# Expert numbers worked out from positions, and one-hot tiles with the row number innermost

## The chip, the cores and the metric

The kernel runs on one core of one Trainium2 chip. The metric is the time in microseconds that the device takes for one execution of the whole program; lower is better. The engines are named as the profile names them: PE is TensorE's matmuls and PEld its weight loads, DVE is VectorE, ACT is ScalarE, POOL is GpSimd (here it only issues gathers while the experts run), SP is SyncE, which issues most plain transfers.

## What is computed

The reference is a two-layer trunk over 512 tokens of width 1024. Each layer has a mixer, which the change leaves alone, and then a layer of experts ("PEER"): 8 heads, each of which picks 16 of 16384 one-neuron experts for every token.

```python
s = jnp.einsum('thpd,hpnd->thpn', q, keys32)               # 8 heads x 2 halves x 128 keys
s1_v, s1_i = lax.top_k(s[:, :, 0, :], 16)
s2_v, s2_i = lax.top_k(s[:, :, 1, :], 16)
cand_v = s1_v[..., :, None] + s2_v[..., None, :]           # 16 x 16 candidates
cand_i = s1_i[..., :, None] * 128 + s2_i[..., None, :]
top_v, top_j = lax.top_k(cand_v.reshape(..., 256), 16)
idx = jnp.take_along_axis(cand_i, top_j, axis=-1)          # 16 expert numbers per head
gate = jax.nn.softmax(top_v, axis=-1)
act = jax.nn.gelu(einsum('thkd,td->thk', u_tab[idx], hb))
out = einsum('thk,thkd->td', gate * act, v_tab[idx])
```

## The kernel before

The tokens stand in four blocks of 128. For the first three blocks (384 tokens) the experts are computed densely: every row of `u` is multiplied with every token, the result is weighted with a gate that is zero for experts not picked, and multiplied with every row of `v`. For the last block the picked rows are gathered from HBM.

**Scores.** `scores(p, ps)` finds, for each of 16 head halves and each token block, the 16 best of 128 keys (`top16`, DVE), with values in `sv` and key numbers in `sx`.

**Selection.** `select(tb)` forms, for the 8 heads of a block, the 50 candidates that can be among the best 16 (list `CAND`: 16 for the best first key, 8 for the second, and so on; `COFF` has the position at which each run begins), values in `cv` and expert numbers in `ci`. `top16` on `cv` gives values `tv` and positions `tj`. The expert number at a position is then looked up one at a time: for each of 8 heads and 16 places one DVE instruction compares a row of 50 position numbers (`iof`) with the position, multiplies with `ci` and sums (line 855, tile `jk`, 128 a block). The sum is split into first and second key number by a shift and a mask. A softmax gives the gate. For blocks 0 to 2 the three tables (first key, second key, gate) are transposed by PE (`pc`) and kept in 16 bits as `slot` and `gh` (the gate in a high and a low part).

**Build.** `build(tb, sel, g8)` makes the dense gate of four tokens. DVE writes one-hot tiles of 128 rows by 128 numbers by 4 tokens, the token innermost: `P` (first key), `Qo` (second key), and two tiles `Q`, which are `Qo` times each part of the gate. PE then multiplies, for each token, `P[:, :, t]` (as weights) with `Q[:, :, t]`, so both are read with a step of four elements: 8 matmuls a group of four tokens (lines 912 and 913), 96 groups a layer. ACT copies the result into `stg`, and every 48 tokens `stg` is written to HBM (`sW`).

**U and V.** `dense_U(i)` multiplies 128 rows of `u` with the 384 tokens: `load_split` brings 512 KB, ACT rounds it (`whi`), DVE takes the rest (`wlo`, line 116), PE makes 24 matmuls of 384 columns (lines 132 to 134), ACT applies GELU (`uo`), and 192 KB go to HBM (`sA`). 128 of these run a layer. After them the working pool `rp` is closed and pool `vp` opened in its place; then for each of 128 groups `A` and `W` are read back, multiplied (DVE), split (`gh`, `gl`), and PE makes 24 matmuls with `v` (lines 1020 to 1022).

**Gathers.** For the last block POOL issues 128 gathers of `u` rows and then 128 of `v` rows, 512 KB each, into three buffers `gr`. DVE consumes each with one instruction of 1024 columns (line 946 for `u`, line 957, tile `gacc`, for `v`). The gathers need `select(3)`, whose numbers become `idi`.

**Order.** The program is written as loops (`select(tb)`, then 32 builds, with a `dense_U` and a gather step at every second one), but a scheduler in the build sets the final order of each engine's instructions ahead of time by its own model of durations. On the chip every engine takes its instructions in that fixed order.

Of the kernel before, what the change touches and what calls it, by code (L numbers as in the profile page):

```python
# [16 lines left out]
T = 512  # L17
# [19 lines left out]
CAND = [16, 8, 5, 4, 3, 2, 2, 2] + [1] * 8  # L37
NCAND = sum(CAND)
COFF = [sum(CAND[:i]) for i in range(16)]


def trunk(tc, a, dbg=None, layers=L, n_i2=128):
    nc = tc.nc
    V, S, G, TE = nc.vector, nc.scalar, nc.gpsimd, nc.tensor
    uid = [0]

    def nm(s):
        uid[0] += 1
        return f"{s}{uid[0]}"
# [3 lines left out]
    cst = ctx.enter_context(tc.tile_pool(name="cst", bufs=1))  # L53
# [19 lines left out]
    it = ctmp.tile([128, 128], I32, name="it")  # L73
# [7 lines left out]
    V.tensor_copy(io4, it[:, :, None].to_broadcast([128, 128, 4]))  # L81
# [400 lines left out]
    def mixer(l, h):  # L482
# [4 lines left out]
        fx = hctx.enter_context(tc.tile_pool(name=f"fx{l}", bufs=1))  # L487
# [8 lines left out]
        G.memset(toe, 0.0)  # L496
        s5_maps(l, sm, fx, hp, ("w1", "w2", "w3"))
        pk0 = pack_tile(fx)
        dcol = fx.tile([128, 32], F32, name=nm("dcol"))
        for j in range(4):  # L500
            nc.sync.dma_start(dcol[32 * j:32 * j + 32, :], a["dsk"][l])
# [227 lines left out]
        fx = mctx.enter_context(tc.tile_pool(name=f"gx{l}", bufs=1))  # L729
# [13 lines left out]
        for e in range(J):  # L743
            ps = proj(40 + e)
# [15 lines left out]
        for e in range(J):  # L760
            later(3)
            ps = dense(a["glu"][l, e], ya)
# [35 lines left out]
    def peer(l, h, rows, gp):  # L798
        pctx = ExitStack()
        rp = pctx.enter_context(tc.tile_pool(name=f"rp{l}", bufs=2))  # L800
# [11 lines left out]
        def scores(p, ps):  # L812
# [9 lines left out]
            for tb in range(NB):  # L822
                wk = rp.tile([128, 128], F32, tag="wk", name=nm("wk"))
                top16(sv[:, tb, p], sx[:, tb, p], s[:, tb], wk)

        def select(tb):
            val = sv[:, tb].rearrange("p (h s) k -> p h s k", s=2)
            idf = rp.tile([128, 16, 16], F32, tag="idf", name=nm("idf"), bufs=1)
            V.tensor_copy(idf, sx[:, tb])
            idv = idf[:].rearrange("p (h s) k -> p h s k", s=2)  # L830
            V.tensor_scalar(idv[:, :, 0, :], idv[:, :, 0, :], 128.0, None, op0=OP.mult)
            cv = rp.tile([128, 8, NCAND], F32, tag="cv", name=nm("cv"), bufs=1)
            ci = rp.tile([128, 8, NCAND], F32, tag="ci", name=nm("ci"), bufs=1)
            for src, dst in ((val, cv), (idv, ci)):
                for r in range(5):
                    n = CAND[r]
                    V.tensor_tensor(dst[:, :, COFF[r]:COFF[r] + n], src[:, :, 0, r:r + 1].to_broadcast([128, 8, n]),
                                    src[:, :, 1, 0:n], op=OP.add)
                V.tensor_tensor(dst[:, :, COFF[5]:COFF[8]].rearrange("p h (r b) -> p h r b", b=2),
                                src[:, :, 0, 5:8, None].to_broadcast([128, 8, 3, 2]),  # L840
                                src[:, :, 1, None, 0:2].to_broadcast([128, 8, 3, 2]), op=OP.add)
                V.tensor_tensor(dst[:, :, COFF[8]:], src[:, :, 0, 8:16],
                                src[:, :, 1, 0:1].to_broadcast([128, 8, 8]), op=OP.add)
            tv = rp.tile([128, 8, 16], F32, tag="tv", name=nm("tv"), bufs=1)
            tj = rp.tile([128, 8, 16], U32, tag="tj", name=nm("tj"), bufs=1)
            for hh in range(8):
                wk = rp.tile([128, NCAND], F32, tag="wk2", name=nm("wk2"))
                top16(tv[:, hh], tj[:, hh], cv[:, hh], wk)
            tf = rp.tile([128, 8, 16], F32, tag="tf", name=nm("tf"), bufs=1)
            V.tensor_copy(tf, tj)  # L850
            code = rp.tile([128, 8, 16], F32, tag="code", name=nm("code"), bufs=1)
# [5 lines left out]
            cint = rp.tile([128, 128], I32, tag="cint", name=nm("cint"), bufs=1)  # L857
            V.tensor_copy(cint, code[:].rearrange("p h k -> p (h k)"))
            ii = rp.tile([128, 2, 128], I32, tag="ii", name=nm("ii"), bufs=1)
            V.tensor_scalar(ii[:, 0], cint, 7, None, op0=OP.logical_shift_right)  # L860
            V.tensor_scalar(ii[:, 1], cint, 127, None, op0=OP.bitwise_and)
            fx = rp.tile([128, 3, 128], F32, tag="fx", name=nm("fx"), bufs=1)
            V.tensor_copy(fx[:, 0:2], ii)

            gv = fx[:, 2].rearrange("p (h k) -> p h k", h=8)
            V.tensor_tensor(gv, tv, tv[:, :, 0:1].to_broadcast([128, 8, 16]), op=OP.subtract)
            S.activation(fx[:, 2], fx[:, 2], AF.Exp)
            zs = rp.tile([128, 8], F32, tag="zs", name=nm("zs"), bufs=1)
            V.tensor_reduce(zs, gv, axis=mybir.AxisListType.X, op=OP.add)
            V.reciprocal(zs, zs)  # L870
            V.scalar_tensor_tensor(gv, gv, GATE, zs[:, :, None].to_broadcast([128, 8, 16]), op0=OP.mult, op1=OP.mult)
            if tb == NB - 1:
                return fx
            pt = ptile([128, 3, 128], "pc")
            for i in range(3):
                TE.transpose(pt[:, i], fx[:, i], ident)
            st = rp.tile([128, 2, 128], F16, tag="slot", name=nm("slot"))
            S.activation(st, pt[:, 0:2], AF.Copy)
            gh = rp.tile([128, 2, 128], F16, tag="gh", name=nm("gh"))
            V.tensor_copy(gh[:, 0], pt[:, 2])  # L880
            V.tensor_tensor(gh[:, 1], pt[:, 2], gh[:, 0], op=OP.subtract)
            return st, gh

        stg = {}
# [1 line left out]
        def build(tb, sel, g8):  # L886
            st, gh = sel
            NT = 4
            c = slice(NT * g8, NT * g8 + NT)
            t0 = 128 * tb + NT * g8  # L890
            n, o = divmod(t0, SG)
            if o == 0:
                stg[0] = rp.tile([128, 128, SG], F32, tag="stg", name=nm("stg"), bufs=2)
            sh = [128, 128, NT]

            def row(t):
                return t[:, None, :].to_broadcast(sh)
# [5 lines left out]
            Qs = []  # L903
            for i in range(2):
                q = rp.tile(sh, F16, tag=f"Q{i}", name=nm("Q"))
                V.tensor_tensor(q, Q_, row(gh[:, i, c]), op=OP.mult)  # L906
                Qs.append(q)
            for b in range(NT // 4):
                ps = ptile([128, 4, 128], "pa")
                for k in range(4):  # L910
                    t = 4 * b + k
                    TE.matmul(ps[:, k], P_[:, :, t], Qs[0][:, :, t], start=True, stop=False)  # L912
                    TE.matmul(ps[:, k], P_[:, :, t], Qs[1][:, :, t], start=False, stop=True)  # L913
# [125 lines left out]
        for i in range(n_end):  # L1039
            w, g = spilled(i)  # L1040
# [31 lines left out]
    for k in ("adab", "n1g", "n2g", "glub"):  # L1072
        sh = a[k].shape
# [51 lines left out]
    for l in range(layers):  # L1125
        h = norm_mod(gain1[l], shift1[l], ssq, G if l == 0 else None)
# [72 lines left out]
```

## Time and profile before

| | us |
|---|---|
| median of 3 runs | 3928.33 (3924.42 to 3931.42) |
| the profiled execution | 3930.45 |
| its span, first to last instruction | 3928.7 |
| PE busy, by the page | 3736.3 |
| DVE busy | 3238.6 |
| ACT busy | 1574.6 |
| POOL busy | 1021.7 |
| data moved | 911.37 MB, mean 232 GB/s |

The two layers look alike: mixer until about 650 us, scores until 770, then a stretch in which U, the selections, the builds and the gathers run together until about 1365, an end of it in which only builds are left, and V from 1436 to 1985; the second layer repeats this some 1935 us later. A matmul's busy time in the profile overlaps with the next one's, so what a matmul costs PE is read from one start to the next. The same holds for DVE instructions that follow each other without a wait. The share "DMA" of a stretch is the mean busy share of the core's 16 DMA engines.

### The profile page before, as it was taken

How to read it: one execution, taken by the hardware profiler on the slowest of the kernel's cores; microseconds unless marked ns; L12 is line 12 of the kernel's file. 1: busy time of each engine (PE TensorE's matmuls, PEld its weight loads, DVE VectorE, ACT ScalarE, POOL GpSimd, SP SyncE). 2: the span in 40 equal slices, each digit the busy share in tenths (PEclk: the TensorE clock that was granted, in tenths of full speed). 3: DMA queues.
4: the chain of work that ended last, by engine and by line, in shares of the span. 5: the costliest groups of instructions: out<-in, count | busy, mean ns of one | idle time of the engine just before them, and what ended most of it. 6: DMA issues, size and time to landing. Idle time of an engine off the chain costs nothing.

```text
span 3928.7 us, 62542 instructions
## 1 busy us (share of the span) xinstructions
PE 3736.3 (95%) x21878; PEld 3502.1 (89%) x21878; DVE 3238.6 (82%) x8715; ACT 1574.6 (40%) x2507; POOL 1021.7 (26%) x1475
## 2 busy tenths in 40 slices
PE   6999999999999959999999999999999997699998
PEld 5888878999999959999988887789999997699998
DVE  6998787999898879877578886679998888787874
ACT  3554443333343323333345554344333433233332
POOL 7454100013222344221033440000232223432210
PEclk9999999999999969999999999999999998899999
DMA  5222384379998989998622225524898898999984
GB/s 197 74 64 78 102 266 143 111 249 318 326 315 304 322 300 351 348 344 315 208 85 75 71 81 168 187 84 136 303 309 315 310 325 289 333 353 344 347 294 134
DMA packets 368764, 911.37 MB, mean 232 GB/s; under 512 B 35824, under 2 KB 187440, under 8 KB 368448
## 3 DMA queue, kind: packets, MB, share of 16 engines
q1 hardware_dynamic: 247696, 536.56, 40.6%
q0 software_dynamic: 73952, 268.56, 19.7%
q10 hardware_dynamic: 46800, 102.26, 6.8%
q8 instruction: 172, 2.82, 0.3%
q14 instruction: 144, 1.18, 0.1%
HBM read 796.09 MB, written 111.15 MB: 231 GB/s over the span
## 4 chain that ended last, share of the span: by engine, by line
PE 77%; DVE 11%; DMA 7%; POOL 2%; issue 2%; ACT 1%; SPq 0%; ACTq 0%; DVEq 0%; POOLq 0%
PE mm L132 12%; PE mm L133 12%; PE mm L134 12%; PE mm L1021 3%; PE mm L1020 3%; PE mm L1022 3%; PE pb L1021 2%; PE pa L1022 2%; PE pb L1020 2%; PE pa L1021 2%; PE pa L1020 2%; PE pb L1022 2%; DMA ada<-ada 2%; DVE wlo L116 2%; PE pa L912 2%; PE pa L913 2%
## 5 line engine op out<-in xcount | busy, mean ns | idle before, releaser
L114 ACT ACTIVATE whi<-raw 128x1024 fp32r<-128x1024 f32 x688 | 728.4, 1060 | 1289.0 <-PE mm L133 751.2
L133 PE MATMUL mm<-alo,whi 128*128 128x384 f32 (+1 forms) x3360 | 1217.2, 363 | 13.6 <-DVE alo L123 13.5
L134 PE MATMUL mm<-ahi,wlo 128*128 128x384 f32 (+1 forms) x3360 | 1216.7, 363 | 10.5 <-DVE wlo L116 10.4
L132 PE MATMUL mm<-ahi,whi 128*128 128x384 f32 (+1 forms) x3360 | 1216.7, 364 | 10.5 <-ACT ahi L229 3.5
L116 DVE TENSOR_TENSOR wlo<-raw,whi 128x1024 fp32r<-128x1024 f32 x688 | 842.1, 1225 | 319.6 <-ACT whi L114 299.5
L133 PEld LDWEIGHTS mm<-alo,whi 128*128 128x128 f32 x3360 | 638.0, 190 | 63.7 <-DVE alo L123 14.8
L134 PEld LDWEIGHTS mm<-ahi,wlo 128*128 128x128 f32 x3360 | 638.1, 190 | 62.6 <-DVE wlo L116 14.0
L132 PEld LDWEIGHTS mm<-ahi,whi 128*128 128x128 f32 x3360 | 638.5, 190 | 61.6 <-ACT ahi L229 4.6
L936 POOL DMA_INDIRECT gr<-ur,idi x256 | 269.5, 1053 | 1481.4 <-DVE jk L855 764.6
L936 POOL DMA_INDIRECT gr<-v,idi x256 | 350.6, 1370 | 669.1 <-DVE gacc L957 583.0
L957 DVE SCALAR_TENSOR_TENSOR gacc<-gr,gate,gacc 128x1024 f32<-128x1024 f32 x254 | 324.5, 1277 | 45.3 <-DMA gr<-v,idi 45.0
L946 DVE SCALAR_TENSOR_TENSOR gr<-gr,rows 128x1024 f32<-128x1024 f32 x256 | 311.1, 1217 | 25.9 <-DMA gr<-ur,idi 24.2
L1021 PE MATMUL mm<-gl,whi 128*128 128x384 f32 x768 | 259.0, 338 | 0.7 <-DVE gl L1011 0.6
L1022 PE MATMUL mm<-gh,wlo 128*128 128x384 f32 x768 | 258.5, 337 | 0.0
L1020 PE MATMUL mm<-gh,whi 128*128 128x384 f32 x768 | 210.0, 338 | 50.6 <-ACT gh L1009 26.4
L1009 ACT ACTIVATE gh<-A 128x384 fp32r<-128x384 f32 x256 | 132.4, 518 | 296.7 <-DVE A L1007 257.8
L912 PE MATMUL pa<-Q,P 128*128 128x128 f16 x768 | 197.7, 296 | 45.2 <-DVE Q L906 42.9
L855 DVE SCALAR_TENSOR_TENSOR jk<-iof,tf,ci 128x50 f32<-128x50 f32 x1024 | 223.8, 262 | 0.0
L914 ACT ACTIVATE stg<-pa 128x512 f32<-128x512 f32 x192 | 114.0, 598 | 220.4 <-PE pa L913 192.2
L913 PE MATMUL pa<-Q,P 128*128 128x128 f16 x768 | 187.9, 295 | 0.9
L1020 PEld LDWEIGHTS mm<-gh,whi 128*128 128x128 f32 x768 | 140.6, 189 | 51.2 <-ACT gh L1009 51.2
L1020 PE MATMUL pb<-gh,whi 128*128 128x384 f32 x512 | 172.8, 338 | 0.0
(382 smaller groups left out, 6642.9 us busy)
## 6 DMA issues: line engine op xcount, KB each, us to landing
raw<-u SPq DMA_DIRECT2D x256, 512.0 KB
raw<-v SPq DMA_DIRECT2D x256, 512.0 KB
raw<-win SPq DMA_DIRECT2D x112, 512.0 KB
ada<-ada SPq DMA_DIRECT2D x96, 512.0 KB
sA<-uo ACTq DMA_DIRECT2D x256, 192.0 KB
sW<-stg ACTq DMA_DIRECT2D x64, 768.0 KB
A<-sA SPq DMA_DIRECT2D x256, 192.0 KB
W<-sW SPq DMA_DIRECT2D x64, 768.0 KB
```

The lines of the kernel that those rows point to most:

```text
L114: S.activation(hi, raw, AF.Copy)
L116: V.tensor_tensor(lo, raw, hi[:].bitcast(F32), op=OP.subtract)
L132: TE.matmul(ps, hi[:, w], ah, start=(j == 0), stop=False)
L133: TE.matmul(ps, hi[:, w], al, start=False, stop=False)
L134: TE.matmul(ps, lo[:, w], ah, start=False, stop=(j == J - 1))
L912: TE.matmul(ps[:, k], P_[:, :, t], Qs[0][:, :, t], start=True, stop=False)
L936: G.indirect_dma_start(out=g[:], out_offset=None, in_=tab, in_offset=bass.IndirectOffsetOnAxis(ap=ids[:, s_:s_ + 1], axis=0))
L946: V.scalar_tensor_tensor(g, g, 1.0, rows, op0=OP.mult, op1=OP.mult, accum_out=dot[:, s_:s_ + 1])
L957: V.scalar_tensor_tensor(acc_, g, gate[:, s_:s_ + 1], acc_, op0=OP.mult, op1=OP.add)
L1020: TE.matmul(ps, w[0][:, c], g[0], start=first, stop=False)
L1021: TE.matmul(ps, w[0][:, c], g[1], start=False, stop=False)
L1022: TE.matmul(ps, w[1][:, c], g[0], start=False, stop=last)
```

## The change

The lookup with `ci` and 128 `jk` instructions a block is replaced by `ranks`, called for four heads at a time. It compares the positions of 64 picks with the 15 places at which the candidate runs begin (`thr`), in one instruction of 960 columns; the flags, times the lengths of the runs (`cnd`) and summed in a tree, give the rank in the second list (`r2`), and the flags, times the differences of neighbouring first key numbers (`step`) and summed, give the first key number. A comparison of `r2` with 16 ranks (`rnk`), times the second key numbers (`second`, made by ACT) and summed, gives the second key number. All of it is in 16 bits, and every operand that is repeated along a row is stored as a pair of equal values, so that the innermost run of each operand is two neighbouring values. The work tiles are the two buffers of tag `s`, which the scores used.

The one-hot tiles now have the row number innermost. `PQ` holds both one-hots of four tokens and is made by one DVE instruction of 1024 columns in place of two of 512; `QQ` holds the two gated ones, two instructions of 512. `slot` and `gh` hold each value as a pair and have one buffer each, not two. PE reads each token's tile as 128 neighbouring elements. The number of matmuls is the same.

```diff
-    io4 = cst.tile([128, 128, 4], F16, name="io4")
+    ioh = cst.tile([128, 64, 2], F16, name="ioh")
...
+    def rank_tables():
+        V.tensor_copy(rnk, iof[:, 0:16, None].to_broadcast([128, 16, 2]))
+        for r in range(1, 16):
+            G.memset(thr[:, r - 1], float(COFF[r]))
+            G.memset(cnd[:, r - 1], float(CAND[r - 1]))
...
+        def ranks(iv, j, o0, o1):
...
+            def pairs(t, n):
+                return t[:, :, None, :].to_broadcast([128, n, 32, 2])
+
+            def twos(w):
+                return w.rearrange("p r (a b) -> p r a b", b=2)
...
+            def total(w, n, o):
+                while n > 2:
+                    m = (n + 1) // 2
+                    V.tensor_tensor(w[:, 0:n - m], w[:, 0:n - m], w[:, m:n], op=OP.add)
+                    n = m
+                V.tensor_tensor(o, w[:, 0], w[:, 1], op=OP.add)
+
+            def gate_rows(w, t, n):
+                sh = [128, n * 4, 8, 2]
+                v = w.rearrange("p r (h a b) -> p (r h) a b", h=4, b=2)
+                V.tensor_tensor(v, v, t[:].rearrange("p r h b -> p (r h) b")[:, :, None, :].to_broadcast(sh), op=OP.mult)
...
+            V.tensor_tensor(twos(ge), twos(j[:, None].to_broadcast([128, 15, 64])), pairs(thr, 15), op=OP.is_ge)
+            V.tensor_tensor(twos(w), twos(ge), pairs(cnd, 15), op=OP.mult)
+            r2 = rp.tile([128, 64], F16, tag="r2", name=nm("r2"), bufs=1)
+            total(w, 15, r2)
+            V.tensor_tensor(r2, j, r2, op=OP.subtract)
+            gate_rows(ge, step, 15)
+            total(ge, 15, o0)
...
+            V.tensor_tensor(twos(eq), twos(r2[:, None].to_broadcast([128, 16, 64])), pairs(rnk, 16), op=OP.is_equal)
+            gate_rows(eq, second, 16)
+            total(eq, 16, o1)
...
-            for hh in range(8):
-                for k in range(16):
-                    jk = rp.tile([128, NCAND], F32, tag="jk", name=nm("jk"))
-                    V.scalar_tensor_tensor(jk, iof[:, 0:NCAND], tf[:, hh, k:k + 1], ci[:, hh], op0=OP.is_equal,
-                                           op1=OP.mult, accum_out=code[:, hh, k:k + 1])
...
+            for hf in range(2):
+                ranks(idv[:, 4 * hf:4 * hf + 4], jf[:, 4 * hf:4 * hf + 4], fx[:, 0, 64 * hf:64 * hf + 64],
+                      fx[:, 1, 64 * hf:64 * hf + 64])
...
-            st = rp.tile([128, 2, 128], F16, tag="slot", name=nm("slot"))
+            st = rp.tile([128, 128, 2, 2], F16, tag="slot", name=nm("slot"), bufs=1)
+            gh = rp.tile([128, 128, 2, 2], F16, tag="gh", name=nm("gh"), bufs=1)
...
-            P_ = rp.tile(sh, F16, tag="P", name=nm("P"))
-            V.tensor_tensor(P_, io4, row(st[:, 0, c]), op=OP.is_equal)
-            Q_ = rp.tile(sh, F16, tag="Qo", name=nm("Qo"))
-            V.tensor_tensor(Q_, io4, row(st[:, 1, c]), op=OP.is_equal)
+            PQ = rp.tile([128, NT, 2, 128], F16, tag="PQ", name=nm("PQ"))
+            V.tensor_tensor(PQ[:].rearrange("p t i (a b) -> p (t i) a b", b=2), ioh[:, None].to_broadcast(sh), pairs(st),
+                            op=OP.is_equal)
+            QQ = rp.tile([128, NT, 2, 128], F16, tag="QQ", name=nm("QQ"))
...
+                V.tensor_tensor(QQ[:, :, i].rearrange("p t (a b) -> p t a b", b=2),
+                                PQ[:, :, 1].rearrange("p t (a b) -> p t a b", b=2),
+                                gh[:, c, i, None].to_broadcast([128, NT, 64, 2]), op=OP.mult)
...
-                    TE.matmul(ps[:, k], P_[:, :, t], Qs[0][:, :, t], start=True, stop=False)
+                    TE.matmul(ps[:, k], PQ[:, t, 0], QQ[:, t, 0], start=True, stop=False)
```

The scheduler, given the new instructions, sets another order. PE before, where the first layer's builds end (`pa` is a build's output, lines 1020 on are V):

```order
L913 MATMUL pa_12622<-Q_12620,P_12614 128x128
L912 LDWEIGHTS P_12614
L912 MATMUL pa_12622<-Q_12618,P_12614 128x128
L913 LDWEIGHTS P_12614
L913 MATMUL pa_12622<-Q_12620,P_12614 128x128
L1020 MATMUL mm_15647<-gh_15666,whi_15657 128x384
L1020 MATMUL mm_15648<-gh_15666,whi_15657 128x384
```

PE now, where they end (lines 142 to 144 are `dense_U`):

```order
L963 MATMUL pa_11499<-QQ_11496,PQ_11494 128x128
L962 LDWEIGHTS PQ_11494
L962 MATMUL pa_11499<-QQ_11496,PQ_11494 128x128
L963 LDWEIGHTS PQ_11494
L963 MATMUL pa_11499<-QQ_11496,PQ_11494 128x128
L142 MATMUL mm_13891<-ahi_6394,whi_13887 128x384
L143 MATMUL mm_13891<-alo_6395,whi_13887 128x384
L144 MATMUL mm_13891<-ahi_6394,wlo_13889 128x384
```

Before, the last 184 build matmuls (23 groups) stand behind the last `dense_U`, and V follows them. Now 136 times three matmuls of `dense_U`, which is 17 of the 128, stand between the last build and the first matmul of V. The first build matmul stood behind 46 `dense_U`; it now stands behind 31.

DVE before, just ahead of the numbers `idi` that the gathers wait for:

```order
L831 TENSOR_SCALAR idf_9606<-idf_9606 128x8x16
L855 SCALAR_TENSOR_TENSOR jk_8140,code_8135<-iof,tf_8133,ci_8068 128x50
L855 SCALAR_TENSOR_TENSOR jk_8142,code_8135<-iof,tf_8133,ci_8068 128x50
L926 TENSOR_SCALAR idx_8485<-idx_8485 128x128
L866 TENSOR_TENSOR fx_8397<-tv_8083 128x128
L926 TENSOR_SCALAR idx_8490<-idx_8490 128x128
L855 SCALAR_TENSOR_TENSOR jk_8144,code_8135<-iof,tf_8133,ci_8068 128x50
L855 SCALAR_TENSOR_TENSOR jk_8146,code_8135<-iof,tf_8133,ci_8068 128x50
L928 CAST idi_8488<-idx_8485 128x128
```

DVE now, at the same place (tiles `s` are the work tiles of `ranks`):

```order
L856 TENSOR_TENSOR fx_7819<-s_7867 128x64
L872 TENSOR_TENSOR s_7948<-s_7947,cnd 128x960
L975 SCALAR_TENSOR_TENSOR idx_8078<-fx_7819 128x128
L975 SCALAR_TENSOR_TENSOR idx_8083<-fx_7819 128x128
L854 TENSOR_TENSOR s_7948<-s_7948 128x448
L861 TENSOR_TENSOR s_7947<-s_7947,step_7943 128x960
L976 TENSOR_SCALAR idx_8078<-idx_8078 128x128
```

Between the last instruction of the scores and the second `idi` DVE had 15 `wlo` and 134 `jk`; it now has 11 `wlo`, no `jk`, and 75 other selection instructions where there were 53. Counted in the same orders, the 128 dot products of the `u` gathers and 27 sums of `v` gathers stood ahead of the first `A` of V; now the 128 dot products and 21 sums do.

## Rows read from the trace of the kernel before

**Rows 1.** Page, parts 1 and 4: engines over the whole span, and the chain by engine.

```profile
PE 3736.3 (95%) x21878; PEld 3502.1 (89%) x21878; DVE 3238.6 (82%) x8715; ACT 1574.6 (40%) x2507; POOL 1021.7 (26%) x1475
...
PE 77%; DVE 11%; DMA 7%; POOL 2%; issue 2%; ACT 1%; SPq 0%; ACTq 0%; DVEq 0%; POOLq 0%
```

**Rows 2.** Windows, first layer: length, busy time (x instructions) by engine, clock, DMA share, GB/s.

```profile
770.00:834.00 64.00, 64.00 (x371) 64.00 (x370) 63.97 (x475) 26.19 (x37) 0.00 (x0) 1.00 0.56 174
834.00:1365.00 531.00, 528.53 (x3211) 512.58 (x3210) 481.76 (x1614) 208.36 (x306) 148.68 (x139) 1.00 0.91 317
1365.00:1436.00 71.00, 24.68 (x170) 18.82 (x169) 53.16 (x109) 14.72 (x26) 36.69 (x20) 0.51 0.81 287
1436.00:1985.00 549.00, 548.29 (x3126) 547.65 (x3125) 419.70 (x664) 198.07 (x261) 129.89 (x100) 1.00 0.87 306
```

**Rows 3.** Windows of 25 us, first layer: one in which the DMA share is 1.00.

```profile
875.00:900.00 25.00, 25.00 (x146) 25.00 (x145) 23.44 (x101) 8.62 (x12) 7.50 (x8) 1.00 1.00 358
```

**Rows 4.** Windows, second layer, from its first gather.

```profile
2768.00:3300.00 532.00, 527.88 (x3211) 510.65 (x3210) 481.82 (x1608) 208.54 (x308) 150.63 (x139) 1.00 0.90 317
```

**Rows 5.** Timeline of PE: start, length in us, line, tile, shape; builds, then U.

```profile
1099.89 0.30 PE L912 MATMUL pa<-Q,P 128*128 128x128 f16 x1
1100.01 0.30 PE L913 MATMUL pa<-Q,P 128*128 128x128 f16 x1
...
1101.09 0.33 PE L134 MATMUL mm<-ahi,wlo 128*128 128x384 f32 x1
1101.26 0.33 PE L132 MATMUL mm<-ahi,whi 128*128 128x384 f32 x1
```

**Rows 6.** Timeline of DVE in the mixer: an instruction of 1024 columns of 32 bits.

```profile
578.30 1.22 DVE L116 TENSOR_TENSOR wlo<-raw,whi 128x1024 fp32r<-128x1024 f32 x1
579.43 0.69 DVE L765 TENSOR_TENSOR sg<-sg,sgb 128x512 f32<-128x512 f32 x1
```

**Rows 7.** Timeline of DVE at the end of the builds.

```profile
1404.91 0.41 DVE L906 TENSOR_TENSOR Q<-Qo,gh 128x512 f16<-128x512 f16 x1
1405.24 0.41 DVE L902 TENSOR_TENSOR Qo<-io,slot 128x512 f16<-128x512 f16 x1
...
1405.91 1.27 DVE L957 SCALAR_TENSOR_TENSOR gacc<-gr,gate,gacc 128x1024 f32<-128x1024 f32 x1
1407.11 0.41 DVE L902 TENSOR_TENSOR Qo<-io,slot 128x512 f16<-128x512 f16 x1
```

**Rows 8.** Timeline of DVE: the end of the scores.

```profile
770.19 0.28 DVE L810 FIND_INDEX8 sx<-sv,wk 128x8 uint32<-128x128 f32 x1
```

**Rows 9.** Timeline of DVE, just ahead of the first gather.

```profile
832.49 0.27 DVE L855 SCALAR_TENSOR_TENSOR jk<-iof,tf,ci 128x50 f32<-128x50 f32 x1
...
832.68 0.27 DVE L855 SCALAR_TENSOR_TENSOR jk<-iof,tf,ci 128x50 f32<-128x50 f32 x1
```

**Rows 10.** Timeline of POOL: the first gather.

```profile
834.14 1.09 POOL L936 DMA_INDIRECT gr<-ur,idi  x1 [385.40 <-DVE zs L869]
```

**Rows 11.** DMA queues from 834 to 1365 us: packets, MB, share of the 16 engines.

```profile
q0 software_dynamic: 19728, 71.84, 41.1%
q1 hardware_dynamic: 15683, 57.11, 30.3%
q10 hardware_dynamic: 18710, 38.53, 18.9%
```

**Rows 12.** Timeline from the last build to the first matmul of V.

```profile
1411.14 0.29 PE L913 MATMUL pa<-Q,P 128*128 128x128 f16 x1
...
1412.09 3.76 ACTq L918 DMA_DIRECT2D sW<-stg  x4
...
1427.45 0.33 SPq L1035 DMA_DIRECT2D A<-sA  x1
...
1434.45 1.03 DVE L1007 TENSOR_TENSOR A<-A,W 128x384 f32<-128x384 f32 x2 [1.63 <-DMA W<-sW]
...
1435.62 1.33 PE L1020 MATMUL mm<-gh,whi 128*128 128x384 f32 x3 [24.19 <-DMA s5s<-ldt]
```

More of the change, by code (lines that the diff above doesn't have):

```diff
@@ L97, in trunk @@
     V.tensor_tensor(eye4, eye4, ident[:, 96:128], op=OP.add)
+    thr = cst.tile([128, 15, 2], F16, name="thr")
+    cnd = cst.tile([128, 15, 2], F16, name="cnd")
+    rnk = cst.tile([128, 16, 2], F16, name="rnk")
+    def rank_tables():
[3 more added lines that the diff above has]
+            G.memset(cnd[:, r - 1], float(CAND[r - 1]))
     def load_raw(src, eng=None):
@@ L498, in mixer @@
         pk0 = pack_tile(fx)
+        if l == 0:
+            rank_tables()
         dcol = fx.tile([128, 32], F32, name=nm("dcol"))
@@ L824, in scores, with work @@
                 top16(sv[:, tb, p], sx[:, tb, p], s[:, tb], wk)
+        def ranks(iv, j, o0, o1):
+            j = j.rearrange("p h k -> p (h k)")
+            def work(n):
+                return rp.tile([128, T], F32, tag="s", name=nm("s"))[:].bitcast(F16)[:, 0:64 * n].rearrange(
+                    "p (r x) -> p r x", r=n)
+            def pairs(t, n):
[12 more added lines that the diff above has]
+                V.tensor_tensor(v, v, t[:].rearrange("p r h b -> p (r h) b")[:, :, None, :].to_broadcast(sh), op=OP.mult)
+            step = rp.tile([128, 15, 4, 2], F16, tag="step", name=nm("step"), bufs=1)
+            two = [128, 4, 15, 2]
+            V.tensor_tensor(step[:].rearrange("p r h b -> p h r b"), iv[:, :, 0, 1:16, None].to_broadcast(two),
+                            iv[:, :, 0, 0:15, None].to_broadcast(two), op=OP.subtract)
+            second = rp.tile([128, 16, 4, 2], F16, tag="second", name=nm("second"), bufs=1)
+            S.activation(second[:].rearrange("p r h b -> p h r b"), iv[:, :, 1, :, None].to_broadcast([128, 4, 16, 2]),
+                         AF.Copy)
+            ge, w = work(15), work(15)
+            V.tensor_tensor(twos(ge), twos(j[:, None].to_broadcast([128, 15, 64])), pairs(thr, 15), op=OP.is_ge)
[5 more added lines that the diff above has]
+            total(ge, 15, o0)
+            o0 = o0.rearrange("p (h k) -> p h k", h=4)
+            V.tensor_tensor(o0, o0, iv[:, :, 0, 0:1].to_broadcast([128, 4, 16]), op=OP.add)
+            eq = work(16)
+            V.tensor_tensor(twos(eq), twos(r2[:, None].to_broadcast([128, 16, 64])), pairs(rnk, 16), op=OP.is_equal)
+            gate_rows(eq, second, 16)
+            total(eq, 16, o1)
@@ L826, in select @@
         def select(tb):
             val = sv[:, tb].rearrange("p (h s) k -> p h s k", s=2)
[L828 removed]
+            idf = rp.tile([128, 16, 16], F16, tag="idf", name=nm("idf"), bufs=1)
             V.tensor_copy(idf, sx[:, tb])
             idv = idf[:].rearrange("p (h s) k -> p h s k", s=2)
[L831 removed]
             cv = rp.tile([128, 8, NCAND], F32, tag="cv", name=nm("cv"), bufs=1)
[L833 removed]
@@ L834, in select @@
-            for src, dst in ((val, cv), (idv, ci)):
+            for src, dst in ((val, cv),):
                 for r in range(5):
@@ L876, in select @@
                 TE.transpose(pt[:, i], fx[:, i], ident)
-            st = rp.tile([128, 2, 128], F16, tag="slot", name=nm("slot"))
[L878 to L881, printed above, removed]
+            st = rp.tile([128, 128, 2, 2], F16, tag="slot", name=nm("slot"), bufs=1)
+            gh = rp.tile([128, 128, 2, 2], F16, tag="gh", name=nm("gh"), bufs=1)
+            for i in range(2):
+                S.activation(st[:, :, i], pt[:, i, :, None].to_broadcast([128, 128, 2]), AF.Copy)
+            g2 = pt[:, 2, :, None].to_broadcast([128, 128, 2])
+            V.tensor_copy(gh[:, :, 0], g2)
+            V.tensor_tensor(gh[:, :, 1], g2, gh[:, :, 0], op=OP.subtract)
             return st, gh
@@ L911, in build @@
                     t = 4 * b + k
-                    TE.matmul(ps[:, k], P_[:, :, t], Qs[0][:, :, t], start=True, stop=False)
-                    TE.matmul(ps[:, k], P_[:, :, t], Qs[1][:, :, t], start=False, stop=True)
+                    TE.matmul(ps[:, k], PQ[:, t, 0], QQ[:, t, 0], start=True, stop=False)
+                    TE.matmul(ps[:, k], PQ[:, t, 0], QQ[:, t, 1], start=False, stop=True)
                 S.activation(stg[0][:, :, o + 4 * b:o + 4 * b + 4], ps[:].rearrange("p t i -> p i t"), AF.Copy,
```

23 lines of the change are left out of this document (6 added, 17 removed).

## The prediction

> **What bounds the kernel now.** I read the page first: PE is busy 95% of the span and makes 77% of the chain that ended last [rows 1]. Windows by stage tell more, because the change touches only one stage, twice. In the first layer that stage runs from the end of the scores at 770 us [rows 8] to the first matmul of V at 1435.6 [rows 12]. Three engines stand close together in it: from the first gather at 834 [rows 10] to 1365 PE is full, DVE is busy 482 of 531 us, and the DMA share is 0.91 [rows 2]. Then, from 1365 to 1436, PE is busy 25 of 71 us at a clock of 0.51, DVE 53: U has run out and the last 23 build groups come at the pace at which DVE writes their one-hots. The last build matmul starts at 1411.1; then `stg` is written, `A` and `W` are fetched when that write has landed (1427.5), and V starts at 1435.6 [rows 12]. V itself, 1436 to 1985, is PE from end to end [rows 2] and is not touched. So the change can give back what is in this stage and no more: the 71 us in which PE mostly waits, PE's time for builds, and the wait for the first gather. The second layer's stretch from its first gather has the same length, 532 us, with a DMA share of 0.90 [rows 4], so I work out one layer and double it.
>
> **PE, part by part.** U: in a window that holds U alone, 146 matmuls start in 25 us [rows 3], 0.171 each, so a `dense_U` of 24 is 4.11 us. Builds start 0.12 apart [rows 5], 768 a layer, 92 us. The new tiles are read as neighbours. No row shows a 16-bit tile read so; the bounds are no change (0.12) and the pace per column of U, 0.171 for 384 columns [rows 5], which is 0.057 for 128. I take 0.065, nearer to the lower end, because the same array takes a column of the U matmuls at that rate; 768 of them are 50 us, 42 less than now.
>
> **DVE, the builds.** An instruction of 512 columns of 16 bits starts 0.33 after the one before [rows 7]; one of 1024 columns of 32 bits takes 1.13 from start to start [rows 6]. So 16 bits go at about double rate already, with operands whose innermost run is four elements. A group costs 4 x 0.33 = 1.32 now and 0.60 to 0.66 + 2 x 0.33 afterwards: nothing is won here if pairs keep the double rate, and over 1 us a group is lost if they don't (a rival below).
>
> **DVE, the lookup.** 128 `jk` a block at 0.19 from start to start [rows 9] are 24.3 us, 97 us a layer. `ranks` has 20 instructions for four heads with some 7600 columns of 16 bits and 310 of 32. At 0.00055 and 0.0011 us a column and 0.06 an instruction (from 0.33 and 1.13 above) that is 4.2 + 0.3 + 1.2 = 5.7 us, 11.4 a block, 46 a layer. Each mostly waits for the one before; up to 0.1 more apiece gives 62. The table `ci`, the shift and the mask, about 15 instructions a block at `jk`'s price, fall away too (11 a layer). DVE so gains 46 to 62 us a layer.
>
> **The first gather.** It waits for `idi`. By the order, 11 `wlo` stand ahead of it after the scores instead of 15. PE needs 4.11 us for each `dense_U` behind them: 11 are 45 us. DVE needs 11 x 1.13, 75 selection instructions of about 0.28, and 82 of the top-16 kind at about 0.12, some 43. I take 48: the first gather comes at 818 instead of 834.
>
> **Who is late next.** From 818 on PE has 115 `dense_U` (the 111 that the 531 us of rows 2 hold beside some 600 build matmuls, and 4 for the 16 us) = 473 us and builds of 50: 523. DVE up to the last build has, counted in the new order, 120 dot products at up to 1.20 (`gacc`'s pace [rows 7]), 95 `wlo` at 1.13, 96 groups at 1.3, and selections of about 50: 425 us, and 17 `dense_U` stand on PE behind the last build, 70 us; no bound. The transfers are. Over 531 us the gather queue moved 71.84 MB in 41.1% of the time of the 16 engines, SP's 57.11 in 30.3%, ACT's 38.53 in 18.9% [rows 11]: 329, 355 and 384 GB/s when they alone are served. In the new stage they have to move 149 gathers of 0.524 MB (237 us), 115 rows of `u` and 4 of `v` (176), and 22.7 MB of `sA` and 25.2 of `sW` (125): 538 us at a share of 1.00. Before, the same stage had 71 us of builds to hide this in. A share of 1.00 occurs, at a full PE [rows 3]; over a whole stage I take 0.98: 549 us. U then ends at 818 + 549 = 1367. V's first `A` and `W` now wait for the last `sA` transfer to land, by the order; before, 24 us lay between the last build and V, of which the landing took 11.6 after the last of four issues and `A`, `W` and their product 8 [rows 12]. One smaller transfer in place of four: 17 us. V starts at 1384 in place of 1435.6, 52 us a layer.
>
> **What costs nothing.** ACT writes `second` and a second `slot` (11 more instructions a layer; it is busy 208 of 531 us [rows 2]). `slot` and `gh` have one buffer, so a block's builds wait for the former block's last; U fills PE there, and without that cover it is a few us, twice a layer. The 30 constants are set by POOL at the start; at POOL's mean of 0.69 us (1021.7 for 1475 [rows 1]) at most 21 us, beside a POOL that is 26% busy and 2% of the chain.
>
> **The sum.** The profiled execution took 3930.45 us, with 3928.7 inside the span; the median of the runs is 2 us lower, which I leave out. 3930 - 2 x 52 = 3826.
>
> **The rivals.**
> *Transfers hide as before or better.* If the share of 1.00 costs PE nothing, PE sets the stage: 523 and 8 of small waits, V at 818 + 531 + 17 = 1366, 70 us a layer: 3790. For it: rows 3.
> *Neighbours buy PE nothing*, so that part of the change doesn't do what it says. Builds stay at 0.12: 473 + 92 + 6 = 571, V at 1406, 30 us a layer: 3870. For it: rows 5 can't tell a step of four from a slow weight load. [...]
> *The share of DMA stays at 0.91*, because DVE takes its instructions in a fixed order and a late gather holds up the `wlo` behind it: 538 / 0.91 = 591, V at 1426, 10 us a layer: 3910. For it: that was the mean while PE was full [rows 2]; against it: PE set the pace then.
> *Pairs lose the double rate* (the other side). An innermost run of two is in no row. At single rate a group costs 1.13 + 2 x 0.60 = 2.33, 98 us a layer more, and `ranks` about 4 more for four heads, 34 a layer: DVE's 425 become some 545, the first gather falls back to 835, the last build to 1380, and 17 `dense_U` and the 17 us follow: V at 1467, 32 us later, 3994. It turns to a loss when DVE's work up to the last build grows by some 100 us, three quarters of that. [...]
>
> **How the numbers follow.** Forecast 0.43; PE sets the stage 0.14; neighbours buy nothing 0.20; the share stays 0.12; pairs at single rate 0.08; within 0.2% (8 us, what a measurement of this kernel can tell from no change) 0.03. Faster: 0.89. The forecast's own range, from 0.96 to 1.00 in share, the landing from 12 to 20 and the first gather 6 either way, is 3800 to 3850. The range takes in PE setting the stage with builds at 0.057 (3777) and some below, and neighbours that buy nothing with some above: 3765 to 3895.
>
> **What would show it.** In the profile after: `PQ` at about 0.60 to 0.66 from start to start and `QQ` at 0.33 (else pairs lost the rate); build matmuls 0.06 to 0.07 apart (else 0.12); the first gather about 48 us after the scores; no stretch of builds alone; V starting some 50 us earlier against its layer's scores, twice, after a wait of 12 to 20 us; a DMA share of 0.95 or more between first gather and V. I am wrong if V itself gets longer, or if DVE waits for gathers while PE waits for `wlo`.

## The result, and the profile after

The changed kernel takes 3859.97 us (median of 4 runs, 3851.53 to 3864.66) against 3929.36 before (4 runs, 3924.42 to 3931.42): a ratio of 0.982, 95% interval 0.980 to 0.984. It is 69 us faster. The forecast was 3826, that is 104 us, so the time is inside the range and a third of the expected gain is missing.

The page of the changed kernel, parts 1 and 4, which answer to [rows 1]:

```profile
PE 3671.6 (95%) x21878; PEld 3436.0 (89%) x21878; DVE 3109.9 (81%) x6700; ACT 1577.9 (41%) x2529; POOL 1043.3 (27%) x1505
...
PE 66%; DMA 13%; DVE 10%; issue 5%; POOL 3%; ACT 2%; ACTq 1%; SPq 0%; DVEq 0%; POOLq 0%
```

PE's share of the chain fell from 77% to 66%, and that of DMA rose from 7% to 13%: something that PE waits for is new. Windows of the changed kernel by stage (length, busy time and instructions by engine, granted clock, DMA share, GB/s), which answer to [rows 2] and [rows 4]:

```profile
775.00:818.00 43.00, 43.00 (x250) 43.00 (x249) 42.90 (x218) 19.81 (x28) 0.00 (x0) 1.00 0.52 180
818.00:1383.00 565.00, 536.51 (x3496) 513.87 (x3494) 472.15 (x944) 229.17 (x346) 177.93 (x146) 0.98 0.90 324
1383.00:1401.00 18.00, 0.12 (x1) 0.12 (x1) 11.10 (x18) 0.74 (x3) 7.92 (x7) 0.54 0.99 349
1401.00:1953.00 552.00, 549.02 (x3125) 548.07 (x3125) 425.86 (x670) 197.80 (x261) 139.08 (x107) 1.00 0.87 309
2715.00:3286.00 571.00, 537.86 (x3491) 514.17 (x3489) 472.30 (x944) 229.07 (x346) 179.04 (x146) 0.98 0.89 320
```

The stretch of builds alone is gone, and the first gather comes 44 us after the scores (818.5 after 774.7) where it came 64 us after [rows 8, 10]. But the stage from first gather to the last U lasts 565 and 571 us, not 549, at a DMA share of 0.90 and 0.89, and PE, which was busy 528.5 of 531 us before, is idle in some 30 us of it. Counted from the end of the scores, V starts 39 us sooner in the first layer (626.2 in place of 665.1) and 36 in the second. Of these 75 us, the spans keep 66 (3862.9 in place of 3928.7): 4 go to a later start of the scores in the first layer (671.0 in place of 666.8; in the other kernels below it was 664.9 to 670.5, so it isn't the change's), 3 to a longer V there, and the rest lies behind V.

What PE waits for is in the list of waits of the changed kernel, 818 to 1400 us (engine, line, waited for: us in all, times, longest):

```profile
ACT uo L800 <- DMA sA<-uo: 28.7, 16, 5.9
...
PE mm L142 <- ACT uo L800: 19.3, 7, 7.3
```

Before, ACT had such waits too, but PE had none for `uo` (list of waits of the kernel before, 834 to 1365 us):

```profile
ACT uo L788 <- DMA sA<-uo: 20.8, 7, 5.7
```

One such wait, in ACT's timeline of the changed kernel (start, length, instruction, and in brackets how long the engine was idle ahead of it and who ended that):

```profile
1302.19 3.13 ACTq L968 DMA_DIRECT2D sW<-stg  x4
...
1306.40 0.85 ACT L800 ACTIVATE uo<-mm 128x384 f32<-128x384 f32 x2
1306.90 1.84 ACTq L801 DMA_DIRECT2D sA<-uo  x2
...
1324.67 0.49 ACT L800 ACTIVATE uo<-mm 128x384 f32<-128x384 f32 x1 [5.88 <-DMA sA<-uo]
```

PE's timeline at the same time:

```profile
1317.54 0.34 PE L144 MATMUL mm<-ahi,wlo 128*128 128x384 f32 x1
1325.21 0.69 PE L142 MATMUL mm<-ahi,whi 128*128 128x384 f32 x1 [7.34 <-ACT uo L800]
1325.70 0.52 PE L143 MATMUL mm<-alo,whi 128*128 128x384 f32 x1
1326.02 0.52 PE L144 MATMUL mm<-ahi,wlo 128*128 128x384 f32 x1
```

ACT issues a block of the gate, four `sW` writes of 786 KB, and right behind them two `sA` writes of 197 KB from the two buffers `uo`. These land some 18 us after their issue (the median of all is 5.2). Until then ACT has no buffer for the next GELU, no `mm` tile comes free, and PE stands still for 7.3 us. Then it starts at half pace: 0.32 from one matmul to the next in place of 0.173. So a stall costs more than its own length, as windows around another one show:

```profile
1180.00:1187.00 7.00, 7.00 (x56) 6.22 (x54) 6.44 (x14) 3.02 (x5) 0.34 (x1) 1.00 1.03 422
1188.00:1192.00 4.00, 0.00 (x0) 0.00 (x0) 3.98 (x8) 0.60 (x2) 0.07 (x1) 0.75 0.97 355
1193.00:1197.00 4.00, 4.00 (x14) 4.00 (x14) 0.52 (x2) 0.49 (x1) 0.94 (x1) 0.52 0.87 264
1198.00:1210.00 12.00, 12.00 (x90) 10.86 (x90) 10.10 (x17) 5.42 (x9) 2.08 (x2) 1.00 0.51 163
```

PE does nothing from 1188 to 1192; the granted clock is then 0.52 while PE is busy again, and 1.00 from 1198 on.

### The profile page after: what moved, and what is told of

Its sections match the earlier page's. It is cut to its first block, busy times and chain, and to the rows that moved or that the text cites. A ratio compares the mean times of both kernels' runs of the same rounds, so it can differ in the third digit from the quotient of the medians.

```text
span 3862.9 us, 60629 instructions
## 1 busy us (share of the span) xinstructions
PE 3671.6 (95%) x21878; PEld 3436.0 (89%) x21878; DVE 3109.9 (81%) x6700; ACT 1577.9 (41%) x2529; POOL 1043.3 (27%) x1505
## 4 chain that ended last, share of the span: by engine, by line
PE 66%; DMA 13%; DVE 10%; issue 5%; POOL 3%; ACT 2%; ACTq 1%; SPq 0%; DVEq 0%; POOLq 0%
PE mm L142 9%; PE mm L143 9%; PE mm L144 9%; DMA sA<-uo 5%; PE mm L1070 4%; PE mm L1071 3%; PE mm L1072 3%; DMA gr<-ur,idi 3%; DMA ada<-ada 2%; PE pa L1072 2%; PE pa L1070 2%; PE pb L1070 2%; PE pa L1071 2%; PE pb L1072 2%; PE pb L1071 2%
## 5 line engine op out<-in xcount | busy, mean ns | idle before, releaser
L986 POOL DMA_INDIRECT gr<-ur,idi x256 | 313.2, 1224 | 1424.4 <-DMA sA<-uo 730.9
L986 POOL DMA_INDIRECT gr<-v,idi x256 | 327.1, 1278 | 691.2 <-DVE gacc L1007 579.4
L1070 PE MATMUL pa<-gh,whi 128*128 128x384 f32 x512 | 172.7, 337 | 0.0
L1072 PE MATMUL pa<-gh,wlo 128*128 128x384 f32 x512 | 172.3, 337 | 0.0
L1071 PE MATMUL pa<-gl,whi 128*128 128x384 f32 x512 | 172.2, 336 | 0.0
L1071 PE MATMUL pb<-gl,whi 128*128 128x384 f32 x512 | 172.0, 336 | 0.0
```

Source lines behind the costliest of these rows:

```text
L986: G.indirect_dma_start(out=g[:], out_offset=None, in_=tab, in_offset=bass.IndirectOffsetOnAxis(ap=ids[:, s_:s_ + 1], axis=0))
L1070: TE.matmul(ps, w[0][:, c], g[0], start=first, stop=False)
L1071: TE.matmul(ps, w[0][:, c], g[1], start=False, stop=False)
L1072: TE.matmul(ps, w[1][:, c], g[0], start=False, stop=last)
```

## Experiments

Three theories for the missing 35 us. **A**: the two `uo` buffers, whose writes land late, stop ACT and with it PE. **B**: the transfers need this time, whatever waits for them. **C**: DVE's fixed order behind late gathers.

**e1: four buffers.**

```diff
-UB = 2
+UB = 4
```

> The changed kernel with four buffers for the GELU output `uo` in place of two, and the order that the scheduler makes with them (12 `dense_U` behind the last build in place of 17; still 31 ahead of the first). In the changed kernel ACT waited 28.7 us a layer for the write of `uo` to land (818 to 1400 us), and PE 19.3 us for ACT's `uo`. Theory A, the two buffers: both waits go to under 5 us, the stage from first gather to last U gets some 20 to 25 us shorter per layer (545 in place of 565), the whole some 3815. Theory B, the transfers need this time whatever waits for them: the waits move to another place (PE for `wlo`, or for `whi`), the stage stays within 5 us a layer, 3860. Theory C, the fixed order of DVE behind late gathers: 3860 too, and PE's waits for DVE grow from 1.4 to 10 us or more.

3790.9 us (4 runs, 3784.0 to 3792.7), 0.965 of before (0.963 to 0.966): another 69 us. Its windows, both layers:

```profile
815.00:1346.00 531.00, 526.72 (x3494) 507.14 (x3492) 463.71 (x938) 225.71 (x346) 173.49 (x138) 1.00 0.94 338
...
2673.00:3215.00 542.00, 530.49 (x3495) 510.08 (x3493) 463.80 (x938) 225.97 (x346) 171.14 (x138) 0.99 0.92 331
```

The same work takes 531 us in place of 565, with PE full, and PE has no wait for `uo` left. By the starts of all matmuls of the first layer's stage, gaps over 0.8 us in U and builds fell from 29 to 3 us, and the time between U matmuls that follow each other without such a gap from 461 to 453, which is the half clock behind the stalls: together the 34 us. B falls: with the same transfers two more buffers are enough for a share of 0.94 and a full PE. C falls as the cause of the loss, since DVE's work and fixed order are much the same, but single places of it remain. The second stage of e1 is 11 us longer than its first; its largest gap, 6 us ahead of a build, begins while DVE waits 5.4 us for gathered rows, with the build's `QQ` behind them in its order (DVE's timeline of e1):

```profile
2842.60 1.23 DVE L996 SCALAR_TENSOR_TENSOR gr<-gr,rows 128x1024 f32<-128x1024 f32 x1 [5.37 <-DMA gr<-ur,idi]
...
2844.89 0.75 DVE L954 TENSOR_TENSOR QQ<-PQ,gh 128x512 f16<-128x512 f16 x2
```

The next gap, 2.8 us, stands behind another such wait (3.2 us). The gain is half as much again as A expected, since I had counted the waits put down to `uo` and not the clock behind them.

**e8: three buffers.**

```diff
-UB = 2
+UB = 3
```

> The changed kernel with three `uo` buffers. The landing of the write takes 5 to 8 us and a `dense_U` 4.1 to 4.6, so three buffers cover two further `dense_U`: theory A (buffers) expects nearly all of what four give, 3790 to 3805, and PE's wait for `uo` under 5 us a layer. If a longer queue of writes is what counts, about half: 3820 to 3830.

3796.0 us (3794.0 to 3797.5). The waits of e8, 815 to 1346 us:

```profile
ACT uo L800 <- DMA sA<-uo: 29.9, 9, 8.1
...
PE mm L142 <- ACT uo L800: 1.2, 1, 1.2
```

ACT waits as long as in the changed kernel, and PE doesn't: one buffer more covers the late landing (1.8 to 20.1 us from issue to landing here, median 5.2). What ACT waits for costs only what reaches PE.

**e9: `sW` on the other queue.** Still two buffers:

```diff
-                    nc.scalar.dma_start(sW[l][n, :, q:q + 32], stg[0][:, q:q + 32])
+                    nc.sync.dma_start(sW[l][n, :, q:q + 32], stg[0][:, q:q + 32])
```

> The changed kernel with two `uo` buffers and one line altered: SP issues the four `sW` writes of 3.1 MB in place of ACT, so that they don't stand on the queue of the `sA` writes (order nearly as in the changed kernel: 31 `dense_U` ahead of the first build, 16 behind the last). In the changed kernel `uo` waits for `sA` right behind a burst of `sW`: four `sW` issued at 1215.9, two `sA` at 1220.1 and 1222.6, and ACT gets its next `uo` at 1237.8; `sA` lands after 4.8 us in the median and 18.7 at most. If the shared queue makes the landing late: the longest landing falls under 8 us, PE's wait for `uo` to under 5 us a layer, and the time comes to 3785 to 3805 without any further buffer. If the two buffers are short whatever stands on the queue: within 10 us of 3860. If the rows of `u` behind `sW` on SP's queue are what then comes late: PE's waits move to `wlo` and `whi`, 3830 or more.

3819.4 us (3812.4 to 3822.3): 41 of the 69 us. The landing of the `sA` writes, in e9 from 818 to 1369 us:

```profile
DMA to landing us min/median/max: 1.9/5.5/11.5
```

In the changed kernel this line reads 1.8, 5.2 and 18.7. PE's waits for `uo` are 7.6 us in place of 19.3 (longest 2.2). So the queue shared with the bursts is the larger part of it. Of what is left, some is still two short buffers (the 7.6 us) and some is builds behind late gathers (PE waits 5.5 us for `QQ`, 0.9 in e1); I had expected one line to do it all. The same line takes some 3 us of issuing for each burst off ACT, which no run sets apart; in e8 ACT still issues them, and the time is within 5 us of e1's. As the order is nearly that of the changed kernel (16 `dense_U` behind the last build, 17 there), these 41 us don't come from another order, which e1 alone couldn't say (it has 12).

**e10: both.**

> Four `uo` buffers and `sW` on SP's queue together. If both remove the same wait, they don't add up: 3785 to 3795, as e1. If SP's queue is the better place anyway, because the last `sA` ahead of V lands sooner: some 5 us a layer less, 3780. If rows of `u` come late behind `sW`: above 3800.

3792.1 us (3790.1 to 3799.4), as e1: both take away the same wait.

**e12: the same line in the kernel before.**

> The kernel before the change with the one line of e9: SP issues the `sW` writes. In the kernel before, ACT waited 20.8 us a layer for `sA` (834 to 1365 us), and PE had no wait for `uo` over 1 us, because builds at 0.118 and the late first build kept PE full. If the late landing of `sA` costs only where PE would otherwise have nothing else to do: no change, 3920 to 3938. If it cost the kernel before as well: 40 us less as in e9, 3890.

3930.4 us against 3930.6, ratio 1.000 (0.999 to 1.001), though ACT's 20.8 us of waits for `sA` ahead of `uo` vanished. This wait was there before the change and cost nothing.

**e2: the lookup alone**, with the former build and one-hots.

```diff
-            PQ = rp.tile([128, NT, 2, 128], F16, tag="PQ", name=nm("PQ"))
...
+            P_ = rp.tile(sh, F16, tag="P", name=nm("P"))
+            V.tensor_tensor(P_, io4, row(st[:, 0, c]), op=OP.is_equal)
```

> Only the lookup by `ranks`; one-hots and builds as before the change (token innermost, PE reads with a step of four). By the order it makes, 31 `dense_U` stand ahead of the first build and 24 behind the last, so there is no stretch of builds alone. Build matmuls at 0.118 in place of 0.056 are 48 us more PE work a layer. Theory A (waits for buffers add to PE's work): 48 us a layer later than the changed kernel, some 3950, slower than before. Theory B (transfers set the stage, PE has about 45 us of slack): within 10 us a layer of the changed kernel, 3860 to 3880, so that the lookup alone carries most of the gain.

3881.3 us (3873.4 to 3883.6), 0.987 of before: 50 of the 69 us. Build matmuls are 0.118 apart. The stage lasts 583 us with PE busy 572. That is about the number of B, but e1 has ruled out its reason: the slower builds cost less than A's 48 us a layer because part of them lies in the time that PE loses to `uo` otherwise (PE's gaps over 0.8 us add up to 11 us a layer, 31 and 36 in the changed kernel).

**e3: the one-hots alone**, with the former lookup.

```diff
-            for hf in range(2):
-                ranks(idv[:, 4 * hf:4 * hf + 4], jf[:, 4 * hf:4 * hf + 4], fx[:, 0, 64 * hf:64 * hf + 64],
...
+            for hh in range(8):
+                for k in range(16):
+                    jk = rp.tile([128, NCAND], F32, tag="jk", name=nm("jk"))
```

> Only the one-hot tiles with the row number innermost; the lookup with 128 `jk` a block. By its order 46 `dense_U` stand ahead of the first build and none behind the last, as before the change. PE's builds fall to 0.056, but the tail of builds alone is set by DVE, whose builds cost the same. If the last build is what V waits for: U ends up to 35 us earlier, the last build where it was, 3915 to 3930. If the builds' pace on PE was itself a bound: some 30 us a layer faster, 3870.

3921.3 us (3916.7 to 3934.1), 0.998 (0.996 to 0.999). Builds are 0.056 apart, U ends 6 us sooner, but the last build starts at 1406 (1411 before): DVE sets the tail. Alone the one-hots give 10 us; beside the lookup, with which the scheduler spreads the builds, they give some 20 (e2 against the changed kernel).

**e4 and e5: a step of four for PE**, with two and with four `uo` buffers.

```diff
+            Pv = PQ[:].rearrange("p t i n -> p (t i n)").rearrange("p (x n f) -> p x n f", n=128, f=4)
+            Qv = QQ[:].rearrange("p t i n -> p (t i n)").rearrange("p (x n f) -> p x n f", n=128, f=4)
...
-                    TE.matmul(ps[:, k], PQ[:, t, 0], QQ[:, t, 0], start=True, stop=False)
+                    TE.matmul(ps[:, k], Pv[:, 0, :, t], Qv[:, 0, :, t], start=True, stop=False)
```

> The changed kernel, but PE reads weights and moving tile of each build with a step of four elements, out of the same tiles (the gate is then made of other numbers, the work is the same). If the step is what made a build matmul 0.118 us long before: 0.118 again in place of 0.056, 48 us more PE work a layer. Theory A: the stage gets longer by all of it, 3950. Theory B: PE's slack of about 45 us a layer takes it, 3860 to 3885. If the pace stays at 0.056, it was the instruction's shape or the order and not the step.

> Four `uo` buffers as in e1 and the step of four of e4 together: PE reads both operands of a build with a step of four elements (the gate is then made of other numbers). With two buffers the step cost 44 us (3903.9 against 3860.0), less than the 2 x 48 that PE has to do more, because part of it filled PE's waits. If PE is what sets the stage once `uo` has four buffers: the step costs all of it, 3790.9 + 96 = 3880 to 3890, and PE is busy all of the stage. If the transfers set the stage (share 0.94 in e1): about half of it is hidden, 3830 to 3850.

e4: 3903.9 us (3896.2 to 3908.4), 44 above the changed kernel. e5: 3865.7 (3864.6 to 3868.0), 75 above e1, with PE busy 528 of 531 us from its first gather on. The pace is 0.118 in both. So the neighbour read is worth 44 us where PE has waits to fill and 75 where it has next to none; the missing 21 of the 96 I put down to the 11 us by which e1's second stage is longer than its first (there was something to fill after all) and to an order that changes between U and builds half as often (70 times in place of 138). Neither was tried apart, but by the starts of the matmuls PE's own work grew by 42 and 38 us in the two layers and not by 48, and the gaps of the second layer fell by 7.

**e6 and e11: which of the two operands**, with four buffers: the step on the weights alone (`Pv` with `QQ`), and on the moving tile alone (`PQ` with `Qv`).

> Four `uo` buffers, and of a build only the weights read with a step of four, the moving tile from neighbours (the gate is then made of other numbers). If the weights' load is what a step slows: build matmuls 0.11 to 0.12 apart, time as e5. If it is the moving tile: 0.056 apart, time as e1, 3790. If both have a part: in between, 0.08.

> Four `uo` buffers; the weights of a build read from neighbours and only the moving tile with a step of four (the gate is then made of other numbers). With the step on the weights alone the pace stayed at 0.056 (e6), with it on both it was 0.118 (e5). If the moving tile's step is the whole cause: 0.118 and the time of e5, 3866. If it takes both steps at once: 0.056 and 3783 to 3791.

e6: 3782.9 us (one run); e11: 3860.2 (one run). PE's timeline of e6:

```profile
1201.65 0.22 PE L965 MATMUL pa<-QQ,PQ 128*128 128x128 f16 x1
1201.71 0.22 PE L964 MATMUL pa<-QQ,PQ 128*128 128x128 f16 x1
1201.76 0.22 PE L965 MATMUL pa<-QQ,PQ 128*128 128x128 f16 x1
```

and of e11:

```profile
1201.34 0.29 PE L965 MATMUL pa<-QQ,PQ 128*128 128x128 f16 x1
1201.46 0.29 PE L964 MATMUL pa<-QQ,PQ 128*128 128x128 f16 x1
1201.57 0.29 PE L965 MATMUL pa<-QQ,PQ 128*128 128x128 f16 x1
```

It is the moving tile: 0.116 with a step of four, 0.056 without; a step on the weights costs next to nothing here (each on one run).

**e7: no pairs** in the one-hots.

```diff
-                return t[:, c].rearrange("p t i b -> p (t i) b")[:, :, None, :].to_broadcast(sh)
+                return t[:, c].rearrange("p t i b -> p (t i) b")[:, :, 0:1].to_broadcast(sh)
```

> The changed kernel (two `uo` buffers), its one-hots made with single values repeated along the row (step of zero innermost) in place of stored pairs; the lookup keeps its pairs. By its order no `dense_U` stands behind the last build (17 in the changed kernel). If the pair is what holds the double rate: `PQ` from 0.60 to 1.13 to 1.20 and `QQ` from 0.335 to 0.60 from start to start, 102 us more of DVE a layer, a stretch of builds alone again, and the time 40 to 100 us above the changed kernel's 3860. If the rate holds without pairs: 0.60 and 0.335, and 3860 give or take 10.

4041.0 us (4039.2 to 4049.9), 181 above the changed kernel and 1.029 of before. DVE's timeline of e7:

```profile
1405.21 1.23 DVE L950 TENSOR_TENSOR PQ<-ioh,slot 128x1024 f16<-128x1024 f16 x1
1406.35 1.29 DVE L1006 SCALAR_TENSOR_TENSOR gacc<-gr,gate,gacc 128x1024 f32<-128x1024 f32 x1
1407.54 1.23 DVE L950 TENSOR_TENSOR PQ<-ioh,slot 128x1024 f16<-128x1024 f16 x1
1408.68 1.30 DVE L955 TENSOR_TENSOR QQ<-PQ,gh 128x512 f16<-128x512 f16 x2
1409.88 1.29 DVE L1006 SCALAR_TENSOR_TENSOR gacc<-gr,gate,gacc 128x1024 f32<-128x1024 f32 x1
```

and the stretch behind its last U:

```profile
1350.00:1463.00 113.00, 35.90 (x255) 25.30 (x255) 108.57 (x124) 18.52 (x32) 82.36 (x30) 0.50 0.60 197
```

`PQ` takes 1.14 from start to start and two `QQ` 1.20, and a tail of builds alone is back, with DVE full. Counted from the end of the scores, V starts 94 and 89 us later than in the changed kernel in the two layers. My expectation for the whole, at most 100 us, was little over half of the 181: I took the 102 us of extra DVE work to be partly hidden, and nothing was left to hide it behind.

## Why the prediction was right, and what was mis-sized

**What the change does was foreseen rightly.** The lookup took its work off DVE and the first gather's way, the tail of builds went, and the builds' pace on PE halved. Point by point, first layer:

| step | predicted | measured |
|---|---|---|
| first gather behind the scores | 48 us | 44 |
| `ranks`, DVE's time a layer | 46 to 62 | 46 |
| build matmul, start to start | 0.065 | 0.056 |
| `PQ`, `QQ`, start to start | 0.60 to 0.66, 0.33 | 0.60, 0.335 |
| PE's own work in the stage, no waits | 523 | 524 in e1 (U 453, builds 36, changes between them 35); 531 here, 8 of it half clock |
| first gather to last U | 549 | 565 (571 in the second layer) |
| last U to V | 17 | 18 |
| V starts sooner, a layer | 52 | 39 and 36 |

Builds of the changed kernel, which answer to [rows 5]:

```profile
1108.16 0.22 PE L963 MATMUL pa<-QQ,PQ 128*128 128x128 f16 x1
1108.22 0.22 PE L962 MATMUL pa<-QQ,PQ 128*128 128x128 f16 x1
```

DVE's one-hots in the changed kernel, which answer to [rows 7]:

```profile
1108.09 0.69 DVE L950 TENSOR_TENSOR PQ<-ioh,slot 128x1024 f16<-128x1024 f16 x1 [0.32 <-PE pa L963]
1108.69 1.22 DVE L996 SCALAR_TENSOR_TENSOR gr<-gr,rows 128x1024 f32<-128x1024 f32 x1
...
1109.84 0.69 DVE L950 TENSOR_TENSOR PQ<-ioh,slot 128x1024 f16<-128x1024 f16 x1
1110.44 1.42 DVE L954 TENSOR_TENSOR QQ<-PQ,gh 128x512 f16<-128x512 f16 x4
```

**The step that failed is the term for the transfers**, 538 us of work at a share of 0.98. Both numbers were off. The queues of the changed kernel from 818 to 1383 us (packets, MB, share of 16 engines), which answer to [rows 11]:

```profile
q0 software_dynamic: 20770, 75.65, 39.6%
q1 hardware_dynamic: 16270, 59.25, 28.5%
q10 hardware_dynamic: 20864, 47.37, 21.8%
```

These shares of 565 us are 224, 161 and 123, in all 508 us of work, 30 less than I had added up: the bytes are those of 144 gathers where I had put 149, 113 rows of `u` and `v` were issued where I had put 119, and the gathers' and SP's queues ran 3 and 4% faster than in [rows 11]. At a share of 0.98 that is 518, under PE's own 524, so by its right size the term would not have set the stage at all. And the share was no limit: e1 has 0.94 in the same stage. I read the 0.91 of the kernel before as transfers that could be packed closer and would then set the pace; there PE was full and set it. The time that I gave the transfers, PE lost to something else. That the time still lies in the stated range, 3765 to 3895, is in part luck. Its upper end came from neighbours that buy PE nothing, which isn't what happened; the forecast's own range, 3800 to 3850, is missed by 10 us; and the share of 0.95 or more that I named as a sign did not show (0.90 and 0.89).

**What took their place** is the wait for `uo`: of 29 and 35 us of gaps in the two layers 21 and 27 stand ahead of a matmul that waited for `uo`. Four buffers take away 26 and 27 (5 in the first layer stood behind late gathers), and 8 and 5 of half clock behind them. It was in the trace of before, as 20.8 us of ACT waiting for `sA`, and I left it out, since PE had no wait there. The prediction should have asked what hid it: builds at 0.118 and a stage in which PE was full, both of which the change takes away. In e12 it costs nothing still; in the changed kernel four buffers give back 69 us.

**The rivals.** *PE sets the stage*, 3790: not the changed kernel's case, but with the wait taken away it is, at 3790.9, by a full PE and a stage of 531. *Neighbours buy PE nothing*: false; undone they cost 44 us (e4). It holds for the weights alone (0.056 with a step of four, e6); on the moving tile a step of four doubles the time from one matmul to the next (0.116, e11). *The share stays at 0.91*: it stayed, but late gathers are the small part of why: PE's waits for `wlo` are 1.3 us in the stage and for `QQ` 5.3, of which 3.3 stand behind a gather that DVE waited 5.7 us for; e1 takes the larger stalls away by buffers alone. *Pairs lose the double rate*: they keep it, and e7 shows the price that they save. The rival had V 83 us behind the forecast's (1467 against 1384) with the lookup slower too; in e7, where the lookup keeps its pairs, V is 94 and 89 behind. The price was too low: the last build comes at 1463 us, not 1380, with no `dense_U` behind it. With a step of zero `PQ` takes 1.14 us from start to start (e7), with stored pairs 0.60.

**The late landing.** e9 ties most of it to the queue: the same `sA` writes, no longer behind `sW`, land within 11.5 us. The packets of ACT's queue in the changed kernel show the order itself: in each of the eight bursts of the first layer those of the two `sA` begin 11 to 15 us after the first of `sW`, when 90 to 97% of those of `sW` have begun (in the last burst `sW` from 1304.3 to 1322.0 us, `sA` from 1318.8). The chain has 17.75 us there from the issue at 1306.9 to the landing. What keeps the longest landing at 11.5 us in e9 wasn't tried.

**Open** is why gathers land late at single places. In e1 two of them, and the half clock behind them, make up most of the 11 us by which the second layer's stage is longer than the first's; what delays them no run here tells.

## What to carry to other kernels

When a change frees an engine that was full, go through the waits of the engines beside it that cost nothing before, and ask for each what hid it: this one was in the first trace. A transfer with few buffers should not share a queue with large bursts (here it landed after up to 18.7 us behind them and 11.5 without), and one buffer more (1.5 KB a partition here) is the cheaper way out: the changed kernel with three `uo` buffers takes 3796 us, with four 3791, and with two and the bursts on the other queue 3819. A DMA share under 1.00 beside an idle engine was no limit of the transfers here (0.90, and 0.94 with more buffers), so try a buffer more before you call it bandwidth.

## What the runs showed of the hardware

- A write of 197 KB issued right behind four of 786 KB on ACT's queue landed after some 18 us (longest 18.7, median of all 5.2); with the large ones on SP's queue the longest was 11.5.
- A matmul of 128 columns of 16 bits starts 0.056 us after the one before if its moving tile is read from neighbours and 0.116 with a step of four; a step of four on the weights leaves 0.056.
- Behind waits of 4.7 and 7.3 us PE ran some 4 and 5 us at a granted clock of 0.52 and 0.51, with 0.32 us from one U matmul to the next in place of 0.173, so that a stall cost more than its length.
- DVE holds the double rate with a value repeated in stored pairs (1024 columns of 16 bits in 0.60 us, of 32 bits in 1.13) and loses it with a step of zero (1.14).
